# A two-block network on one core: the first block's mixer with float32 projections, modulation vectors as TensorE products, and the whole convolution on VectorE

## The chip, the core and the metric

The kernel runs on one core of a Trainium2 chip: TensorE (PE, with PEld for its weight loads), VectorE (DVE), ScalarE (ACT) and GpSimd (POOL), and one queue of DMA issues on SyncE (SP). The metric is the device time of one execution in microseconds (us); it is given as the median of several runs. A profile is one further execution.

## What is computed

256 tokens of width 1024 go through two blocks. The change touches the first half of the first block, the mixer:

```
mod = silu(c) @ ada_w + ada_b              # 6 vectors of 1024: shift, scale, gate (mixer), shift, scale, gate (ffn)
u   = rmsnorm(x) * (1 + sc_mix) + sh_mix
p   = u @ w_in                             # 8 tiles of 128 columns for the conv, 14 for rwkv
y_conv = silu(layernorm(conv31(a * sigmoid(b)) + b_dw))     # 31 taps, 512 channels, causal
y_rwkv = rwkv7(p_rwkv)                     # decaying 64x64 state per head, group norm, bonus, gate
x   = x + gt_mix * ([y_conv, y_rwkv] @ w_out)
u   = rmsnorm(x) * (1 + sc_ffn) + sh_ffn
x   = x + gt_ffn * peer_ffn(u)             # 8 heads, top 16 of 128 x 128 experts
```

A second block follows (two attention branches, a gated merge and a feed-forward part).

## The kernel before

The tokens are two tiles of 128 (t=0, 1). Each float32 weight tile is loaded by one DMA on SP (512 KB) into a ring (`W_wraw`, three buffers), then split: `wload` casts it to a high part (`W_whi`, on ACT or DVE) and subtracts for a low part (`W_wlo`, on DVE). The activations are split likewise (`Au_uhi`, `Au_ulo`; `Amix_mixhi`, `Amix_mixlo`), and each product is three matmuls in fp32r: high by high, low by high, high by low.

The first block's mixer, called the head here, runs in this order. `norm_T` normalises x and computes `u` for pairs of its eight 128-row blocks. Ahead of each pair, `mods` gets four tiles of the modulation: multiply by silu(c) and sum along the row, three on DVE (`An_mraw`, one instruction with an accumulator) and one on POOL with the sum on ACT. After each pair, `proj_blocks` adds that pair's share of six rwkv tiles ("side", `w_side`). `proj` then does the other eight rwkv tiles (`w_rwkv`) and the eight conv tiles (`w_conv`); each rwkv tile gets its token shift on DVE (`Afeat_xs`). `prep` makes decay, keys and gates. For four chunks of 64 tokens, DVE fills `Ach_W` and `Ach_ZR`, PE multiplies them, and DVE masks the result (`Ach_AB`). The 16x16 blocks on the diagonal go out to DRAM and back (`scrn`, `Ach_nblk`); `base` inverts them on DVE in 15 steps of a multiply (`Ach_ublkp`) and a reduce (`Ach_ublk`); the result goes out (`scrx`) and comes back as `Arw_XT`. `chunk_mats` doubles the inverse in two levels (masked copies COPY_PREDICATED on DVE, `Arw_X`, `Arw_XT`), `chunk_state` carries the state over the chunks (`Arw_VS`, `Arw_S0f`), and `rwkv_out` finishes a token tile: group norm (`Aprep_yr`, `Afeat_gno`), bonus and gate.

`conv` sums 31 taps for four groups of 128 channels into `Afeat_cacc`: group 0 on PE with diagonal matrices (`Arw_cdiag`, 31 float32 matmuls and eight DMAs), groups 1 and 2 on DVE (60 multiply-adds), group 3 as ACT products and POOL sums. The 24 late modulation tiles (vectors 2, 3, 4) are multiplied on DVE or POOL and summed on ACT or DVE. `tok_mm` multiplies by `w_out` (13 tile loads: 8 for t=0, 5 again for t=1), and `E_gtmp` multiplies by the gate. Behind the head come the queries, the top-k and experts of the first block, and the second block.

The order on each engine is fixed ahead of the run by a list scheduler: every operation has a cost, a readiness and a priority (a table of offsets by part, operation and tile), and each engine's queue takes the best ready one. The engines then run their queues strictly in order; so does SP with its DMAs. In the rows of profile and order all operations have one line, that of a helper; names of tiles tell them apart.

## Time and profile before

| | before |
|---|---|
| median of three runs | 1544.62 us (1543.45 to 1553.45) |
| profiled execution | 1536.19 us, span 1534.4 us |
| PE busy | 1413.9 us, 92% |
| DVE busy | 1319.7 us, 86% |
| ACT, POOL busy | 570.0 us, 158.9 us |
| DMA | 305.14 MB, mean 199 GB/s |
| head: last gate multiply of the mixer starts at | 264.18 us |

A busy share says how much of a stretch an engine had work in progress; matmuls are pipelined, so their single durations overlap, and the spacing of their starts is their price.

### The profile page before, as it was taken

Reading aid. Unit: us, or ns where it says so; the run is one execution under the profiler, and the core shown is the slowest. Engines: PE = TensorE matmul, PEld = TensorE weight load, DVE = VectorE, ACT = ScalarE, POOL = GpSimd, SP = SyncE. Lnnn points to the kernel's source line nnn. Section 1 sums busy time; section 2 is a strip of 40 time slices with the busy share of each in tenths; the row PEclk is TensorE's granted clock in tenths of the full one; section 3 lists DMA queues with packets and bytes.
Section 4 is the critical chain, followed back from the end, with each engine's and each line's share of the span. In section 5 each row is a group of like instructions: output and inputs, shape, how many; then the busy total and the mean of one; then the engine's idle time right before and its main releaser. Section 6 shows DMA issues by size and latency. Waiting matters only on the chain.

```text
span 1534.4 us, 24599 instructions
## 1 busy us (share of the span) xinstructions
PE 1413.9 (92%) x9309; PEld 1256.7 (82%) x9309; DVE 1319.7 (86%) x2402; ACT 570.0 (37%) x1019; POOL 158.9 (10%) x127
## 2 busy tenths in 40 slices
...
GB/s 320 252 137 162 165 104 179 230 157 159 114 151 184 134 153 164 174 165 171 208 286 273 303 297 297 293 294 261 197 177 193 157 152 150 221 220 192 193 179 138
DMA packets 99224, 305.14 MB, mean 199 GB/s; under 512 B 17952, under 2 KB 24864, under 8 KB 98976
## 3 DMA queue, kind: packets, MB, share of 16 engines
...
q14 instruction: 47, 0.39, 0.1%
...
## 4 chain that ended last, share of the span: by engine, by line
PE 56%; DVE 24%; DMA 12%; issue 4%; ACT 3%; SPq 0%; POOL 0%; DVEq 0%; ACTq 0%
PE bank L693 56%; DVE W_wlo L693 8%; DVE W_whi L693 2%; DMA W_wraw<-in_peer_v_dram 2%; DVE Afeat_cacc L693 1%; ACT W_whi L693 1%; DMA A_mraw<-in_wmodT_dram 1%; DMA W_wraw<-in_w_out_dram 1%; DMA row<-A_rowcol 1%; DVE Bt_pos L693 1%; DVE Bt_tix L693 1%; DVE Ach_ZR L693 1%; DVE A_mraw L693 1%; DVE Bt_tv L693 1%; DMA row<-C_rowcol 1%
## 5 line engine op out<-in xcount | busy, mean ns | idle before, releaser
L693 DVE TENSOR_TENSOR W_wlo<-W_wraw,W_whi 128x1024 fp32r<-128x1024 f32 (+1 forms) x456 | 560.8, 1236 | 43.4 <-ACT W_whi L693 27.4
L693 ACT CAST W_whi<-W_wraw 128x1024 fp32r<-128x1024 f32 (+1 forms) x238 | 248.8, 1047 | 263.4 <-PE bank L693 162.5
L693 PE MATMUL bank<-X_u2hi,W_wlo 128*128 128x256 f32 x1088 | 302.0, 288 | 12.1 <-DVE W_wlo L693 11.8
L693 PE MATMUL bank<-X_u2hi,W_whi 128*128 128x256 f32 x1088 | 302.6, 287 | 1.7 <-DVE W_whi L693 0.9
L693 PE MATMUL bank<-X_u2lo,W_whi 128*128 128x256 f32 x1088 | 299.7, 285 | 0.0
L693 PEld LDWEIGHTS bank<-X_u2hi,W_wlo 128*128 128x128 f32 x1088 | 205.8, 193 | 15.5 <-DVE W_wlo L693 15.4
L693 DVE CAST W_whi<-W_wraw 128x1024 fp32r<-128x1024 f32 (+1 forms) x218 | 149.4, 686 | 73.1 <-PE bank L693 53.3
L693 PEld LDWEIGHTS bank<-X_u2hi,W_whi 128*128 128x128 f32 x1088 | 206.3, 193 | 2.6 <-DVE W_whi L693 1.5
L693 PEld LDWEIGHTS bank<-X_u2lo,W_whi 128*128 128x128 f32 x1088 | 206.1, 193 | 0.0
L693 PE MATMUL bank<-W_whi,A_ah 128*128 128x512 f32 x512 | 138.7, 390 | 3.9 <-ACT A_ah L693 3.0
L693 PE MATMUL bank<-W_whi,A_al 128*128 128x512 f32 x512 | 139.1, 391 | 1.2 <-DVE A_al L693 1.1
L693 PE MATMUL bank<-W_wlo,A_ah 128*128 128x512 f32 x512 | 138.8, 390 | 1.3 <-DVE W_wlo L693 1.3
L693 PEld LDWEIGHTS bank<-W_whi,A_ah 128*128 128x128 f32 x512 | 95.8, 188 | 25.0 <-ACT A_ah L693 3.6
L693 PEld LDWEIGHTS bank<-W_wlo,A_ah 128*128 128x128 f32 x512 | 95.9, 188 | 22.7 <-DVE W_wlo L693 3.0
L693 PEld LDWEIGHTS bank<-W_whi,A_al 128*128 128x128 f32 x512 | 95.7, 188 | 22.9 <-DVE A_al L693 3.1
L693 ACT CAST A_ah<-gH_gH 128x256 fp32r<-128x256 f32 x128 | 51.2, 406 | 157.7 <-PE bank L693 151.1
L693 PE MATMUL bank<-C_chi,W_wlo 128*128 128x256 f32 (+1 forms) x424 | 106.2, 285 | 0.4 <-DVE W_wlo L693 0.3
L693 PE MATMUL bank<-C_clo,W_whi 128*128 128x256 f32 (+1 forms) x424 | 104.6, 283 | 0.0
L693 PE MATMUL bank<-C_chi,W_whi 128*128 128x256 f32 (+1 forms) x424 | 104.1, 282 | 0.0
L693 DVE SCALAR_TENSOR_TENSOR A_mraw<-A_mraw,A_cvec 128x1024 f32<-128x1024 f32 x56 | 68.3, 1220 | 11.2 <-DMA A_mraw<-in_wmodT_dram 6.0
L693 PEld LDWEIGHTS bank<-C_chi,W_wlo 128*128 128x128 f32 (+1 forms) x424 | 73.8, 187 | 1.8 <-DVE W_wlo L693 1.0
L693 POOL TENSOR_TENSOR C_cosg<-C_rope,C_gains 128x128 f32<-128x128 f32 x8 | 5.6, 730 | 657.9 <-DVE A_mraw L693 652.8
...
## 6 DMA issues: line engine op xcount, KB each, us to landing
W_wraw<-in_peer_u_dram SPq DMA_DIRECT2D x128, 512.0 KB, 3.3
W_wraw<-in_peer_v_dram SPq DMA_DIRECT2D x128, 512.0 KB, 4.5
...
```

The lines of the kernel that those rows point to most:

```text
L693: return getattr(eng, "tensor_copy" if meth == "copy" and e != "ACT" else meth)(*args, **kw)
```

## The change

**Projections.** `u` is kept in float32 (`Au_u`); `u` and the weight tiles of `w_side`, `w_rwkv`, `w_conv` and `w_out` are not split any more. Each product is one float32 matmul from the loaded tile: 176 matmuls with 256 columns in place of 528 in fp32r, and 32 with 512 columns in place of 96. The loads alternate between two rings of three buffers (`Afeat_hraw`, `W_wraw`). `w_out` is loaded once (8 tiles); the conv rows (k 0 to 3) are multiplied first for both token tiles, the rwkv rows (k 4 to 7) for t=0 and then t=1.

**Modulation.** Of the four tiles ahead of a pair, one is now eight float32 products with one column each on PE; three stay on DVE. The late vectors 2, 3 and 4 are eight loads each (`adaR`, 24 in all), each with four matmuls of one output row and 256 columns, which write PSUM partitions 0, 32, 64 and 96; then a copy on ACT, two transposes and one addition on DVE. POOL has no multiplies left in the head.

**Convolution.** All four groups run on DVE: 120 multiply-adds and four first taps. The diagonal matrices and their DMAs are gone.

**Order.** The table of priorities is tuned anew for the whole kernel, and the scheduler's costs of one-row and small matmuls and its rule on POOL and DVE sharing a port are changed. From the queries on, the same instructions remain but for two more table loads on ACT and a few elementwise ones that moved from DVE to POOL; their order differs in places.

The diff, without the table of priorities:

```diff
@@ load and modulation helpers @@
+    def wload32(self, ap, n=1024):
+        self.ring += 1
+        raw = self.T("Afeat", "hraw", [1024], F32, 3) if self.ring % 2 else self.T("W", "wraw", [1024], F32, WRAW)
+        self.nc.sync.dma_start(raw[:, 0:n], ap)
+        return raw[:, 0:n]
+    def mod_products(self, nts, load, tag="m", z=None):
+        nc = self.nc
+        ps = self.psum(tag)
+        for n, nt in enumerate(nts):
+            w = load(self.a["adaN"][nt])
+            for k in range(KT):
+                nc.tensor.matmul(ps[:, n:n + 1], w[:, k * P:(k + 1) * P], self.ccol[:, k:k + 1], start=k == 0, stop=k == KT - 1)
+        return ps
+    def mod_rows(self, i):
+        nc = self.nc
+        ps = self.psum("m")
+        z = self.zero
+        nc.tensor.matmul(ps[:, 0:256], z[:, 0:P], z[:, 0:256], start=True, stop=False)
+        for k in range(KT):
+            w = self.wload32(self.a["adaR"][i, k])
+            for g in range(4):
+                nc.tensor.matmul(ps[32 * g:32 * g + 1, 0:256], self.ccol[:, k:k + 1], w[:, g * 256:(g + 1) * 256], start=False,
+                                 stop=False)
+        nc.tensor.matmul(ps[:, 0:256], z[:, 0:P], z[:, 0:256], start=False, stop=True)
+        rows = self.T("Afeat", "modrows", [256])
+        nc.scalar.copy(rows[:], ps[:, 0:256])
+        pt = self.psum("m")
+        for q in range(2):
+            nc.tensor.transpose(pt[:, q * P:(q + 1) * P], rows[:, q * P:(q + 1) * P], self.ident[:])
+        o = self.mod[:, 0, 8 * i:8 * i + 8].rearrange("p (g q) -> p q g", q=2)
+        b = self.colr("ada_b", 8 * i, 8).rearrange("p (g q) -> p q g", q=2)
+        nc.vector.tensor_add(o, pt[:, 0:256].rearrange("p (q g e) -> p q g e", q=2, e=32)[:, :, :, 0], b)
...
@@ norm_T @@
+        if both:
+            u32 = self.T(oregion, name, [KT, S])
-                nc.any.affine(u[:, q * w:(q + 1) * w], ps[:, q * w:(q + 1) * w], sc[:, k:k + 1], shcol[:, k:k + 1])
+                nc.any.affine(u32[:, k] if both else u[:, q * w:(q + 1) * w], ps[:, q * w:(q + 1) * w], sc[:, k:k + 1], shcol[:, k:k + 1])
+            if both:
+                if split:
+                    nc.scalar.copy(hi[:, sl], u32[:, sl])
+                    nc.vector.tensor_sub(lo[:, sl], u32[:, sl], hi[:, sl].bitcast(F32))
+                after(k0, (u32, hi, lo) if split else (u32,))
+                continue
             uv = u[:].rearrange("p (k t) -> p k t", k=nk)
...
@@ first projections @@
+    def mm_feat(self, ps, ap, u, full, start=True):
+
+        if not full:
+            return self.mm3_feat(ps, self.wload(ap), u[1], u[2])
+        w = self.wload32(ap)
+        for k in range(KT):
+            self.nc.tensor.matmul(ps, w[:, k * P:(k + 1) * P], u[0][:, k], start=k == 0, stop=k == KT - 1)
-            whi, wlo = net.wload(net.a["w_side"][k], SIDE * P)
+            w = net.wload32(net.a["w_side"][k], SIDE * P) if SIDE32 else net.wload(net.a["w_side"][k], SIDE * P)
             for n in range(SIDE):
-                ps = self.pw[n // 2][:, n % 2 * S:(n % 2 + 1) * S]
-                b = slice(n * P, (n + 1) * P)
-                nc.tensor.matmul(ps, whi[:, b], hi[:, k], start=False, stop=False)
-                nc.tensor.matmul(ps, whi[:, b], lo[:, k], start=False, stop=False)
-                nc.tensor.matmul(ps, wlo[:, b], hi[:, k], start=False, stop=k == KT - 1 and n % 2 == 1)
+                ps, b = self.pw[n // 2][:, n % 2 * S:(n % 2 + 1) * S], slice(n * P, (n + 1) * P)
+                sp = k == KT - 1 and n % 2 == 1
+                for x, y in ((w, u[0]),) if SIDE32 else ((w[0], u[1]), (w[0], u[2])):
+                    nc.tensor.matmul(ps, x[:, b], y[:, k], start=False, stop=sp and SIDE32)
+                if not SIDE32:
+                    nc.tensor.matmul(ps, w[1][:, b], u[1][:, k], start=False, stop=sp)
-                net.mm3_feat(half(ps, q), net.wload(w), hi, lo)
+                net.mm_feat(half(ps, q), w, u, RWKV32 if x >= 0 else CONV32)
...
@@ conv @@
-        nc.bias = CONV_BIAS
-        pe = net.psum("x") if CONV_PE else None
-        for k in range(CONV_PE):
-            if k % 4 == 0:
-                dg = net.T("Arw", "cdiag", [4, P], F32, 2)
-                n = min(4, CONV_PE - k)
-                nc.sync.dma_start(dg[:, :n], net.a["conv_diag"][:, k * P:(k + n) * P].rearrange("p (k e) -> p k e", e=P))
-            nc.tensor.matmul(pe[:, :S], dg[:, k % 4], self.convy[:, 0, k:k + S], start=k == 0, stop=k == CONV_PE - 1)
-        nc.bias = 0.0
         nc.bias = TAP_BIAS
         for c in range(4):
-            for k in range(CONV_PE if c == 0 else 0, TAPS):
+            for k in range(TAPS):
                 w = net.col("conv_dw_w", c * TAPS + k)
                 src = self.convy[:, c, k:k + S]
                 if k == 0:
                     nc.vector.tensor_scalar(acc[:, c], src, w, net.col("conv_dw_b", c), op0=OP.mult, op1=OP.add)
-                elif c < CONV_DVE:
-                    nc.vector.scalar_tensor_tensor(acc[:, c], src, w, pe[:, :S] if c == 0 and k == CONV_PE else acc[:, c],
-                                                   op0=OP.mult, op1=OP.add)
                 else:
-                    tp = net.T("Afeat", "tap", [S], F32, 2)
-                    nc.scalar.activation(tp[:], src, AF.Copy, scale=w)
-                    nc.gpsimd.tensor_tensor(acc[:, c], acc[:, c], tp[:], op=OP.add)
-            if c == 0 and CONV_PE:
-                nc.scalar.activation(acc[:, 0], pe[:, :S] if CONV_PE == TAPS else acc[:, 0], AF.Identity, bias=net.col("conv_dw_b", 0))
+                    nc.vector.scalar_tensor_tensor(acc[:, c], src, w, acc[:, c], op0=OP.mult, op1=OP.add)
...
@@ first_mix @@
+    def early(ap):
+        w = net.T("An0", "mraw1", [D], F32, 2)
+        nc.sync.dma_start(w[:], ap)
+        return w
     def mods(k0):
-        net.mod_tiles(0, (k0, k0 + 8, k0 + 1, k0 + 9), FIRST_ENG, "An0", "mraw0", 6)
-        z = lambda ap: ap.rearrange("p (z k) -> p z k", z=2)[:, :, k0:k0 + 2]
-        m = z(net.mod[:, 0, 0:16])
-        net.nc.vector.tensor_add(m, m, z(net.colr("ada_b", 0, 16)))
-    hi, lo = net.norm_T("An0", "Au", net.xs, net.colr("norm_mix_g"), net.mod[:, 0, 0:8], net.mod[:, 0, 8:16], "u", "x",
-                        before=mods, after=mx.proj_blocks)
-    mx.proj(hi, lo)
-    nc = net.nc
-    nc.part = "mods"
-    nc.bias = MOD_BIAS
-    spare = {"c": ("Afeat", "cacc", [4, S]), "y": ("Aprep", "yr", [4, S]), "a": ("Ach", "AB", [4, S], F32, 4)}
-    net.mod_tiles(0, range(16, 16 + MOD_EARLY), MOD_ENG0, spare=[spare[x] for x in MOD_SPARE],
-                  after=net.mod[:, 0, MOD_AFTER:MOD_AFTER + 1])
-    nc.bias = 0.0
+        nts = (k0, k0 + 1, k0 + 8, k0 + 9)
+        if MOD_PE0:
+            ps = net.mod_products(nts[:MOD_PE0], early)
+            for n, nt in enumerate(nts[:MOD_PE0]):
+                nc.vector.tensor_add(net.mod[:, 0, nt:nt + 1], ps[:, n:n + 1], net.colr("ada_b", nt, 1))
+        net.mod_tiles(0, nts[MOD_PE0:], ("vector",), "An0", "mraw0", 5)
+        for nt in nts[MOD_PE0:]:
+            net.mod_bias(0, nt, nt + 1)
+    u = net.norm_T("An0", "Au", net.xs, net.colr("norm_mix_g"), net.mod[:, 0, 0:8], net.mod[:, 0, 8:16], "u", "x",
+                   before=mods, after=mx.proj_blocks, split=not (SIDE32 and RWKV32 and CONV32))
+    mx.proj(u)
     nc.bias = PREP_BIAS
     mx.prep()
     nc.bias = 0.0
@@ -2173,13 +2261,15 @@
     mx.base()
     mx.turn_v()
     M = mx.chunk_mats(0)
+    for i in (2, 3, 4):
+        nc.part = f"mods{i}"
+        nc.bias = MOD_BIAS
+        net.mod_rows(i)
+        nc.bias = 0.0
     mx.bonus()
     mx.conv()
-    nc.part = "mods late"
-    net.mod_tiles(0, range(16 + MOD_EARLY, 40), MOD_ENG)
-    net.mod_bias(0, 16, 40)
-    mx.split_mix(mx.acc, 0, slice(0, S))
     w_out = net.a["w_out"]
+    mix = [mx.acc[:, k] for k in range(4)] + [mx.y[:, k] for k in range(4)]
     for c in range(4):
         M, M1 = mx.chunk_mats(c + 1) if c < 3 else None, M
         nc.bias = STATE_BIAS
@@ -2187,18 +2277,28 @@
         nc.bias = 0.0
         if c == 1:
             mx.rwkv_out(0)
-            mx.split_mix(mx.y, 4, slice(0, P))
         if c == 2:
             mx.ps = [[net.psum(tag) for h in range(2)] for tag in "uv"]
             nc.part = "out0"
-            kept = tok_mm(net, mx.mhi, mx.mlo, w_out, mx.ps, [4, 5, 6, 7, 0, 1, 2, 3], (0,))
+            w = []
+            for k in range(8):
+                w.append(net.wload32(w_out[k]))
+                out_products(net, mix, w, mx.ps, (0, 1) if k < 4 else (0,), (k,))
     nc.bias = OUT_BIAS
     mx.rwkv_out(1)
-    mx.split_mix(mx.y, 4, slice(P, S))
     nc.bias = 0.0
     nc.part = "out1"
-    tok_mm(net, mx.mhi, mx.mlo, w_out, mx.ps, [1, 2, 3, 0, 4, 5, 6, 7], (1,), kept=kept)
+    out_products(net, mix, w, mx.ps, (1,), range(4, 8))
     return mx
+def out_products(net, x, w, ps, tt, ks):
+    for k in ks:
+        for t in tt:
+            for h in range(2):
+                net.nc.tensor.matmul(ps[t][h][:], x[k][:, t * P:(t + 1) * P], w[k][:, h * 512:(h + 1) * 512],
+                                     start=k == 0, stop=k == 7)
```

Where the order moves, on SP first: the end of the base, before. `Ach_ublk` is the base's result, `scrx0` to `scrx3` its four pieces in DRAM, `Arw_XT` the tile it comes back to.

```order
L693 DMA Arw_cdiag_0_1282<-in_conv_diag_dram 128x512
L693 DMA scrx0<-Ach_ublk_0_466 32x16x16
L693 DMA scrx1<-Ach_ublk_0_466 32x16x16
L693 DMA scrx2<-Ach_ublk_0_466 32x16x16
L693 DMA scrx3<-Ach_ublk_0_466 32x16x16
L693 DMA Arw_XT_0_1276<-scrx0 128x4x128
L693 DMA Arw_XT_1_1277<-scrx1 128x4x128
L693 DMA Arw_cdiag_1_1283<-in_conv_diag_dram 128x512
L693 DMA W_wraw_1_82<-in_adaT_dram 128x1024
```

And in the changed kernel; `in_adaR_dram` holds the late modulation weights.

```order
L696 DMA scrx0<-Ach_ublk_0_400 32x16x16
L696 DMA scrx1<-Ach_ublk_0_400 32x16x16
L696 DMA scrx3<-Ach_ublk_0_400 32x16x16
L696 DMA Afeat_hraw_2_109<-in_adaR_dram 128x1024
L696 DMA scrx2<-Ach_ublk_0_400 32x16x16
L696 DMA W_wraw_2_84<-in_adaR_dram 128x1024
...
L696 DMA W_wraw_2_84<-in_adaR_dram 128x1024
L696 DMA Afeat_hraw_2_109<-in_adaR_dram 128x1024
L696 DMA W_wraw_1_83<-in_adaR_dram 128x1024
L696 DMA Arw_XT_0_923<-scrx0 128x4x128
L696 DMA Arw_XT_1_924<-scrx1 128x4x128
L696 DMA W_wraw_0_82<-in_adaR_dram 128x1024
```

Before, the two reads of `scrx` follow the four writes directly; now twelve loads of `adaR` stand between the write of `scrx0` and its read.

On DVE, from the last base steps to the first masked copies, before (`Afeat_cacc` is the convolution's sum):

```order
L693 TENSOR_TENSOR Ach_ublkp_0_467<-Ach_ublk_0_466,Ach_nblk_0_465 128x225
L693 TENSOR_REDUCE Ach_ublk_0_466<-Ach_ublkp_0_467 128x15
L693 SCALAR_TENSOR_TENSOR Afeat_cacc_0_105<-Afeat_convy_0_104,G_cols_0_72,Afeat_cacc_0_105 128x256
...
L693 COPY Arw_VS_0_1270<-bank3_63 64x4x64
L693 TENSOR_TENSOR Aprep_av_0_120<-bank0_60,Afeat_xs_0_103 128x512
...
L693 TENSOR_SCALAR Afeat_cacc_0_105<-Afeat_convy_0_104,G_cols_0_72 128x256
L693 TENSOR_SCALAR Aprep_av_0_120<-Aprep_av_0_120,G_cols_0_72 128x256 x4
L693 SCALAR_TENSOR_TENSOR Aprep_yr_0_119,G_mod_0_77<-Aprep_yr_0_119,Afeat_cvec_0_93 128x1024
...
L693 COPY_PREDICATED Arw_X_0_1274<-Afeat_clev_0_95,bank4_64 128x16x16
L693 COPY_PREDICATED Arw_XT_0_1276<-Afeat_clev_0_95,bank3_63 128x16x16
L693 SCALAR_TENSOR_TENSOR Afeat_cacc_0_105<-Afeat_convy_0_104,G_cols_0_72,Afeat_cacc_0_105 128x256
L693 COPY_PREDICATED Arw_XT_0_1276<-Afeat_clev_0_95,bank3_63 128x8x32
```

And in the changed kernel:

```order
L696 TENSOR_TENSOR Ach_ublkp_0_401<-Ach_ublk_0_400,Ach_nblk_0_399 128x225
L696 TENSOR_REDUCE Ach_ublk_0_400<-Ach_ublkp_0_401 128x15
L696 TENSOR_SCALAR Afeat_cacc_0_111<-Afeat_convy_0_106,G_cols_0_72 128x256 x2
L696 SCALAR_TENSOR_TENSOR Afeat_cacc_0_111<-Afeat_convy_0_106,G_cols_0_72,Afeat_cacc_0_111 128x256 x11
...
L696 SCALAR_TENSOR_TENSOR Afeat_cacc_0_111<-Afeat_convy_0_106,G_cols_0_72,Afeat_cacc_0_111 128x256 x36
L696 TENSOR_TENSOR Afeat_convy_0_106<-bank0_60,Au_convsg_1_139 128x256
L696 TENSOR_SCALAR Afeat_cacc_0_111<-Afeat_convy_0_106,G_cols_0_72 128x256
...
L696 COPY Arw_VS_1_918<-bank4_64 64x4x64
...
L696 SCALAR_TENSOR_TENSOR Afeat_cacc_0_111<-Afeat_convy_0_106,G_cols_0_72,Afeat_cacc_0_111 128x256 x17
L696 COPY_PREDICATED Arw_X_0_921<-Afeat_clev_0_97,bank4_64 128x16x16
L696 SCALAR_TENSOR_TENSOR Afeat_cacc_0_111<-Afeat_convy_0_106,G_cols_0_72,Afeat_cacc_0_111 128x256 x4
L696 COPY_PREDICATED Arw_XT_0_923<-Afeat_clev_0_97,bank3_63 128x16x16
```

Two of the convolution's multiply-adds stood ahead of the third masked copy; now 66 stand ahead of the first one, and the others lie between the masked copies, state copies and sums that follow.

On PE, around the transposes of the second token tile's group norm (`Afeat_gno`), before:

```order
L693 MATMUL bank4_64<-W_whi_1_85,Amix_mixhi_0_1265 128x512
L693 MATMUL bank3_63<-W_whi_1_85,Amix_mixhi_0_1265 128x512
L693 MATMUL bank0_60<-G_ident_0_74,Afeat_gno_0_115 128x128 x4
L693 MATMUL bank4_64<-W_wlo_0_87,Amix_mixhi_0_1265 128x512
L693 MATMUL bank3_63<-W_wlo_0_87,Amix_mixhi_0_1265 128x512
L693 MATMUL bank4_64<-W_whi_1_85,Amix_mixlo_0_1266 128x512
L693 MATMUL bank3_63<-W_whi_1_85,Amix_mixlo_0_1266 128x512
L693 MATMUL bank4_64<-W_whi_0_84,Amix_mixhi_0_1265 128x512
```

And in the changed kernel:

```order
L696 MATMUL bank0_60<-Afeat_cmask_0_96,Afeat_gsq_0_115 128x8 x4
L696 MATMUL bank3_63<-W_wraw_0_82,Aprep_yr_0_130 128x512
...
L696 MATMUL bank4_64<-W_wraw_2_84,Aprep_yr_0_130 128x512
L696 MATMUL bank3_63<-W_wraw_2_84,Aprep_yr_0_130 128x512
L696 MATMUL bank2_62<-G_ident_0_74,Afeat_gno_0_119 128x128 x4
L696 MATMUL bank6_66<-Afeat_hraw_1_108,Afeat_cacc_0_111 128x512
...
L696 MATMUL bank5_65<-W_wraw_1_83,Afeat_cacc_0_111 128x512
L696 MATMUL bank6_66<-Afeat_hraw_0_107,Aprep_yr_0_130 128x512
L696 MATMUL bank5_65<-Afeat_hraw_0_107,Aprep_yr_0_130 128x512
...
L696 MATMUL bank5_65<-W_wraw_2_84,Aprep_yr_0_130 128x512
```

Before, split products of t=0 (banks 3 and 4) lie on both sides of the transposes; now all of t=0 stands in front of them, and 12 float32 products of t=1 (banks 5 and 6) behind, the last eight with `Aprep_yr`.

## Rows read from the trace of the kernel before

**Rows 1.** Page, part 1: busy us (share of the span) and instructions.

```profile
PE 1413.9 (92%) x9309; PEld 1256.7 (82%) x9309; DVE 1319.7 (86%) x2402; ACT 570.0 (37%) x1019; POOL 158.9 (10%) x127
```

**Rows 2.** Stretches: length; busy us of PE, PEld, DVE, ACT, POOL; clock.

```profile
0.00:57.20 57.20, 24.43 (x150) 21.63 (x151) 44.27 (x87) 20.20 (x36) 12.22 (x14) 1.00 0.81 295
57.20:123.00 65.80, 56.53 (x390) 53.00 (x389) 63.99 (x108) 36.00 (x60) 12.44 (x15) 0.95 0.54 181
...
152.00:200.00 48.00, 46.00 (x471) 41.07 (x472) 30.97 (x54) 33.10 (x68) 38.30 (x25) 1.00 0.56 177
200.00:228.00 28.00, 18.54 (x96) 14.42 (x96) 26.33 (x67) 5.04 (x10) 0.00 (x0) 0.63 0.18 53
228.00:265.00 37.00, 31.39 (x132) 23.68 (x131) 33.36 (x56) 18.14 (x29) 1.05 (x1) 0.91 0.54 180
265.00:1534.00 1269.00, 1219.92 (x7962) 1087.76 (x7962) 1096.62 (x1982) 444.49 (x794) 75.69 (x53) 0.99 0.60 201
```

**Rows 3.** Group on DVE, 0 to 265 us: count | busy, mean ns.

```profile
L693 DVE MEMSET Ach_ZR<- 128x1024 f32 x4 | 3.6, 912 | 0.6 <-issue 0.5
```

**Rows 4.** Stretch, DVE on tiles W_wlo and W_whi alone (casts, splits).

```profile
57.20:123.00 65.80, 16.62 (x15) 0.95 0.54 181
```

**Rows 5.** DVE in order of time (start, length), 44 to 58 us.

```profile
44.73 1.22 DVE L693 SCALAR_TENSOR_TENSOR An_mraw<-An_mraw,Afeat_cvec 128x1024 f32<-128x1024 f32 x1
...
57.27 0.88 DVE L693 SCALAR_TENSOR_TENSOR Afeat_xs<-bank,Afeat_omu,Au_shift 128x256 f32<-128x256 f32 x2
```

**Rows 6.** PE in order of time, 42 to 44 us.

```profile
42.04 0.84 PE L693 MATMUL bank<-Au_uhi,W_whi 128*128 128x256 f32 x3
...
43.56 0.28 PE L693 MATMUL bank<-Au_ulo,W_whi 128*128 128x256 f32 x1
43.68 0.29 PE L693 MATMUL bank<-Au_uhi,W_wlo 128*128 128x256 f32 x1
```

**Rows 7.** DVE in order of time, 122 to 184 us.

```profile
122.26 0.68 DVE L693 TENSOR_TENSOR Ach_AB<-bank,Afeat_cmask 128x512 f32<-128x512 f32 x1
...
133.34 0.80 DVE L693 TENSOR_TENSOR Ach_ublkp<-Ach_ublk,Ach_nblk 128x1 f32<-128x1 f32 x1 [2.21 <-DMA Ach_nblk<-scrn]
...
137.84 0.17 DVE L693 TENSOR_TENSOR Ach_ublkp<-Ach_ublk,Ach_nblk 128x16 f32<-128x16 f32 x1
...
138.93 0.57 DVE L693 TENSOR_TENSOR Ach_ublkp<-Ach_ublk,Ach_nblk 128x36 f32<-128x36 f32 x1
...
150.84 0.39 DVE L693 TENSOR_REDUCE Ach_ublk<-Ach_ublkp 128x15 f32<-128x225 f32 x1
...
162.33 0.44 DVE L693 COPY_PREDICATED Arw_X<-Afeat_clev,bank 128x256 f32<-128x256 uint8 x1 [0.70 <-PE bank L693]
...
183.49 0.69 DVE L693 TENSOR_TENSOR Aprep_yr<-Aprep_yr,bank 128x512 f32<-128x512 f32 x1
```

**Rows 8.** POOL in order of time, 136 to 153 us.

```profile
136.24 16.84 POOL L693 TENSOR_TENSOR Afeat_cacc<-Afeat_cacc,Afeat_tap 128x256 f32<-128x256 f32 x19 [2.12 <-DVE Ach_ublkp L693]
```

**Rows 9.** SP's queue in order of time, 122 to 131 us.

```profile
122.97 0.38 SPq L693 DMA_DIRECT2D scrn<-Ach_AB  x1
...
130.06 0.33 SPq L693 DMA_DIRECT2D Ach_nblk<-scrn  x1
```

**Rows 10.** DVE in order of time, 200 to 266 us.

```profile
201.20 13.54 DVE L693 SCALAR_TENSOR_TENSOR Afeat_cacc<-Afeat_convy,G_cols,Afeat_cacc 128x256 f32<-128x256 f32 x34
...
225.23 0.68 DVE L693 TENSOR_TENSOR Aprep_yr<-Aprep_yr,bank 128x512 f32<-128x512 f32 x1
...
264.18 1.28 DVE L693 TENSOR_TENSOR E_gtmp<-bank,E_row 128x512 f32<-128x512 f32 x2
```

**Rows 11.** PE in order of time: float32 products, 256 columns and 1 column.

```profile
193.42 1.03 PE L693 MATMUL bank<-Afeat_convy,Arw_cdiag 128*128 128x256 f32 x4
194.28 0.27 PE L693 MATMUL bank<-G_ident,Afeat_gno 128*128 128x128 f32 x1
...
230.29 2.91 PE L693 MATMUL bank<-Afeat_o,Afeat_convy 128*128 128x1 f32 x16 [1.67 <-ACT Afeat_convy L693]
```

893 lines of the change are left out of this document (469 added, 424 removed).

## The prediction

> **What bounds the kernel now.** I read the busy shares first. PE is busy 92% of the span and DVE 86% [rows 1], which looks like a PE-bound kernel; by stretch it is not so. From 265 us to 1534 us PE works 1219.9 of 1269 us [rows 2], and the change leaves those instructions as they are. In the head PE works 24.4 of the first 57.2 us, while DVE works 44.3; from 57.2 to 123 us DVE works 64.0 of 65.8 us; from 200 to 228 us DVE works 26.3 of 28 while PE works 18.5 at a granted clock of 0.63 [rows 2]. So the head is led by DVE and by chains that pass through it, and only its last 37 us, where PE works 31.4, are led by PE.
>
> Then I took DVE in order of time and noted when each stage ends: the first token shift at 57.27, the last masked AB at 122.26, the base from 133.34 to 151.23, the first masked copy at 162.33, the mean subtraction of the first group norm at 183.49 [rows 5, 7]; the same of the second group norm at 225.23 and the last gate multiply at 264.18 [rows 10]. The sum below moves these marks one by one.
>
> **The first shift.** What goes: the fp32r casts and splits of `u` and `w_side`, which ended between the last modulation multiply at 44.73 and the shift at 57.27 [rows 5]. What stays: sixteen modulation tiles of 0.52 MB, eight side tiles of 0.39 MB and about 1.5 MB of inputs, 13 MB. The stretch moved 295 GB/s [rows 2], at which 13 MB take 44 us. DVE has 12 of the 1.2 us multiplies left and almost nothing between them, so the data sets the pace. PE adds 32 one-column products: eight of them took 2.91 us [rows 11], 11.6 us in all, in a stretch in which it idles 33. The 48 side products in float32 cost 0.43 us each (two of them, four records, from 193.42 to 194.28 [rows 11]), and only the last pair's twelve, 5 us, lie behind the last modulation tile. I take 45 us: 12 saved, or 6 if the side products run at the half speed that split ones showed up to 43 us (three in 0.84 us, against starts 0.12 us apart just behind [rows 6]).
>
> **From the shift to the base.** DVE's 64.0 us held 16.6 of weight casts and splits [rows 4] and, as the program has it, five late modulation multiplies of 1.2 us. Without both it has 41. Three of the four ZR clears of 0.9 us [rows 3] go to POOL: 38 to 39. PE must put through 47 float32 projections (20 us), eight lora and sixteen ZR by W products of the same form (10 us) and small ones before the last AB: about 36 us, nearly as much. Table loads on ACT and two engines so close in length will not fit without a gap; I take 43 us for the stage and keep the 11.1 us from the last AB to the first base step, of which the write to `scrn` took 7.1 until its read was issued [rows 7, 9]. Base start: 45 + 43 + 10 = 98, against 133.34. Saved in this stage 23, with ends of 27 (39 us) and 15.
>
> **The base.** It took 17.9 us for 15 steps. While POOL summed the convolution from 136.24 to 153.08 [rows 8], a multiply of 36 elements took 0.57 us and one of 16 just before took 0.17 [rows 7]; the casts and other work in between took some 4 us. POOL has nothing left to do then. At 0.17 us and a little for the longer steps, 15 pairs take 7 to 9 us; I take 9, which saves 9. The other end is 14 us, if the two multiplies of `Afeat_convy` that stand ahead of step 15 wait: their 32 float32 products, 14 us, start behind the last AB product at about 88 and end near 103, when step 15 is due. Base end: 107 against 151.23.
>
> **Base to first group norm.** Here the change gives time back. All of the convolution now stands on DVE between the base and that subtraction: 120 multiply-adds, 0.396 us apart (34 of them from 201.20 to 214.66 [rows 10]), and four first taps of about 0.5: 49.5 us. That is the price of taps back to back while POOL rests, as it does in the changed kernel. Twenty-odd other instructions there (six masked copies of 0.44 [rows 7], state copies, sums, bonus) make 13 us. DVE has 63 us in a row and comes to the subtraction at 170; before it took 32.3. Lost: 31, or 36 with waits at the small ones. The late modulation hides under this: 24 loads of 0.52 MB take 43 us at 295 GB/s, from about 107 to 150, and `Arw_XT`, behind twelve of them on SP, lands at about 128. DVE does not reach the first masked copy before 66 taps and four first taps are done, 107 + 28 + 3 = 138, so ten microseconds cover it. If that cover were gone, every further microsecond would move the chunk chain.
>
> How long the one-row products take no row shows. Serially, 96 of 0.43 us are 41 us on PE; if the four that go to different partitions run side by side, 10 us. PE has some 60 us here and little else, so I charge nothing, but at the upper end each load's four take 1.7 us and the loads go no slower than the 1.8 us that their DMA takes. The Trainium skill, TensorEngine Tiling (Array Packing), section Key Properties, says that tiles operate independently and can multiply in parallel, and also that changing the tiling mode drains TensorE; by the first the 96 cost 10 us, by the second each return to full-width products adds a drain that no row of this trace prices. The sum is the same by either.
>
> **First to second group norm.** Before: 41.7 us, of which 53 taps took 21 on DVE, in front of state copies. None are left, so 21 remain for the two last chunks. PE has 24 float32 w_out products of 512 columns in there or just behind, 0.85 us each by twice the 256 column price: 20 us, of which I let 6 fall on the chain. 27 us: 15 saved, between 8 and 20.
>
> **Second group norm to the last gate multiply.** Before: 39.0 us, during which split w_out products kept PE full and five weight tiles were split. Now: about 6 us until the normalised tile is ready (an estimate: a dozen small steps on DVE, ACT and PE, 0.2 to 0.7 us each), five products ahead of its transposes (4 us, partly under it), twelve behind them at 0.85, 10 us; the first four, with convolution rows, cover the 3 us of bonus and gate. 19 us at full clock, 33 at half; PE falls to 0.63 in a like stretch, 200 to 228 us [rows 2]. I take 22: 17 saved, between 6 and 20. The Trainium skill, TensorE: Matmul & The Clock Gate, section What's actually happening, has it that the throttled state is the default and that activity releases it; by that alone the products would start at half speed wherever PE waits for the state chain, and the end would lie near 33 us, not 22. Rows of this case show both: 0.63 where DVE held the chain, 0.91 from 228 on.
>
> **The sum.** 12 + 23 + 9 - 31 + 15 + 17 = 45. I have costed each stage as if its longest engine ran without gaps; before, even the stretch full of taps idled 6% and the chunk stretch, 152 to 200, idled 17 of 48 us on DVE [rows 2]. Six per cent of the 125 us from the first shift to the first group norm are 8 us, so the head ends 37 us sooner. Against the profiled execution's 1536.2 us that is 1499; the median of the runs was 1544.6, and on that scale it is 1508.
>
> **Rivals.** *The convolution on DVE takes back most of the gain* (small gain). For: 49.5 us of taps in an in-order queue ahead of masked copies, with `Arw_XT` behind twelve loads on SP. If one-row products run serially at half clock, 3.4 us a load, twelve loads end at 148, not 128, and the first masked copy at 150, not 138; with state copies waiting behind taps for 8 us more, the gain is 37 - 20 = 17: 1528. Against: the taps themselves fill the wait.
>
> *The tail pays.* Its order is retuned; PE idles 49 of 1269 us there [rows 2], so at most 49 can be won, and an order that adds a third to this idle time loses 16: 1524. Against: instruction counts and the load order there hardly differ.
>
> *Slower: float32 products on a half-speed PE.* From the shift to the last AB, PE needs 36 us at full clock and DVE 39; at half clock PE needs 72 and leads. Then the base starts at 127 in place of 98, `convy` comes 14 us later still, the last stage takes 33 us in place of 22: 29 + 14 + 11 = 54, and the result is 1508 + 54 = 1562. It decides from about 50 us of float32 work at half clock, since 37 are then used up. For: the half speed up to 43 us [rows 6]. Against: the clock is 0.95 in this stage [rows 2], and PE will be busier in it than before.
>
> *No effect.* The marks move, but the clock or waits take about 35 us at the head's end: 1543.
>
> **Chances.** My forecast, gain of 22 to 55 us: 0.60. More than that: 0.05. Small gain or a paying tail: 0.19, about half of it over 1%. No effect: 0.08. Slower: 0.08. One per cent, about what a measurement here can tell from no change, is 15 us; faster by more: 0.75, within: 0.17, slower by more: 0.08. The best ends of all terms (12, 27, 10, -28, 20, 20) sum to 61; the worst (6, 15, 4, -36, 8, 6) to 3: 1484 to 1541 holds a little over eight tenths.
>
> **What would show it.** In the new profile: first shift at 45, last AB at 88, base from 98 to 107, the masked copy near 138 behind taps, the two subtractions at 170 and 197, the last gate multiply near 225; group of taps 0.40 us each; no POOL multiply in the head; and the stretch behind the head as long as before, 1269 us. The forecast is wrong if PE's clock lies near 0.5 before 100 us, if a masked copy waits for `Arw_XT`, or if that last stretch changes by over 10 us.

## The result and the profile after

The changed kernel takes 1504.51 us (median of four, 1502.66 to 1507.02) against 1545.6 beside it: a ratio of 0.973, interval 0.970 to 0.976, 41 us faster. The prediction said 1508, between 1484 and 1541, and faster by over 1% with a chance of 0.75. The profiled execution took 1507.02 us, span 1505.2. Its page, part 1, and the first line of its chain of waits:

```profile
PE 1432.8 (95%) x9307; PEld 1252.0 (83%) x9307; DVE 1258.5 (84%) x2395; ACT 511.3 (34%) x917; POOL 97.8 (6%) x91
...
PE 72%; DVE 14%; DMA 9%; ACT 3%; issue 2%; SPq 0%; POOL 0%; DVEq 0%; ACTq 0%; POOLq 0%
```

By stretches (length; busy us of PE, PEld, DVE, ACT, POOL; granted clock, DMA share, GB/s), cut where the stages end now:

```profile
0.00:43.50 43.50, 33.33 (x163) 28.88 (x164) 25.45 (x78) 10.10 (x21) 9.25 (x16) 1.00 0.94 367
43.50:96.00 52.50, 50.81 (x242) 43.19 (x241) 43.88 (x92) 21.77 (x39) 2.61 (x14) 1.00 0.52 153
96.00:106.00 10.00, 10.00 (x48) 8.81 (x47) 9.00 (x33) 0.38 (x1) 0.00 (x0) 1.00 0.35 118
106.00:181.00 75.00, 63.52 (x577) 44.80 (x576) 60.09 (x153) 14.03 (x32) 0.00 (x0) 0.95 0.68 227
181.00:213.00 32.00, 32.00 (x264) 23.91 (x263) 14.03 (x38) 12.47 (x22) 0.00 (x0) 0.95 0.15 50
213.00:232.00 19.00, 19.00 (x60) 9.44 (x58) 12.20 (x29) 3.02 (x8) 0.00 (x0) 1.00 0.22 63
232.00:1505.00 1273.00, 1224.13 (x7964) 1092.98 (x7962) 1093.87 (x1978) 449.58 (x796) 85.91 (x61) 0.99 0.62 201
```

Before, DVE led most of the head [rows 2]; now each stretch has its own leader: DMA up to 43.5 us (0.94 busy), PE from there to the base, and PE again from 181 us on (51 of 51 us). Only from 106 to 181 us is no engine full: PE 63.5 of 75, DVE 60.1, DMA 0.68. The question behind the result lies there. DVE in order of time shows the marks that the prediction named:

```profile
43.48 0.88 DVE L696 SCALAR_TENSOR_TENSOR Afeat_xs<-bank,Afeat_omu,Au_shift 128x256 f32<-128x256 f32 x2 [1.11 <-ACT Au_shift L696]
...
85.12 2.48 DVE L696 TENSOR_TENSOR Ach_AB<-bank,Afeat_cmask 128x512 f32<-128x512 f32 x4
...
96.00 0.16 DVE L696 TENSOR_TENSOR Ach_ublkp<-Ach_ublk,Ach_nblk 128x1 f32<-128x1 f32 x1 [2.32 <-DMA Ach_nblk<-scrn]
...
98.06 0.22 DVE L696 TENSOR_TENSOR Ach_ublkp<-Ach_ublk,Ach_nblk 128x36 f32<-128x36 f32 x1
...
105.39 0.39 DVE L696 TENSOR_REDUCE Ach_ublk<-Ach_ublkp 128x15 f32<-128x225 f32 x1
...
132.46 6.92 DVE L696 SCALAR_TENSOR_TENSOR Afeat_cacc<-Afeat_convy,G_cols,Afeat_cacc 128x256 f32<-128x256 f32 x17
141.26 0.45 DVE L696 COPY_PREDICATED Arw_X<-Afeat_clev,bank 128x256 f32<-128x256 uint8 x1 [1.88 <-PE bank L696]
...
180.28 0.69 DVE L696 TENSOR_TENSOR Aprep_yr<-Aprep_yr,bank 128x512 f32<-128x512 f32 x1 [4.27 <-PE bank L696]
...
212.81 0.69 DVE L696 TENSOR_TENSOR Aprep_yr<-Aprep_yr,bank 128x512 f32<-128x512 f32 x1 [1.98 <-PE bank L696]
...
230.45 0.69 DVE L696 TENSOR_TENSOR E_gtmp<-bank,E_row 128x512 f32<-128x512 f32 x1 [0.60 <-PE bank L696]
```

They answer to [rows 5, 7, 10]. At the masked copy and at both group norms DVE now waits for PE, where the prediction had PE wait for DVE's taps.

What PE and SP did around `Arw_XT` (the base's result, read back), in order of time:

```profile
126.98 3.19 PE L696 MATMUL bank<-Au_u,W_wraw 128*128 128x256 f32 x14
130.11 0.61 PE L696 MATMUL bank<-W_wraw,G_ccol 128*1 128x256 f32 x8
...
134.91 0.63 PE L696 MATMUL bank<-G_ident,Arw_XT 128*128 128x128 f32 x4 [0.68 <-DMA Arw_XT<-scrx]
...
150.71 0.61 PE L696 MATMUL bank<-Afeat_hraw,G_ccol 128*1 128x256 f32 x8 [1.90 <-DMA Afeat_hraw<-in_adaR_dram]
151.14 0.61 PE L696 MATMUL bank<-W_wraw,G_ccol 128*1 128x256 f32 x8
151.68 0.94 PE L696 MATMUL bank<-Arw_X,Ach_AB 128*128 128x128 f32 x6
...
162.17 1.10 PE L696 MATMUL bank<-Arw_R,Arw_XT 128*128 128x64 f32 x8
...
168.11 1.00 PE L696 MATMUL bank<-Arw_R,Arw_XT 128*128 128x64 f32 x8
...
176.39 1.06 PE L696 MATMUL bank<-G_ident,Arw_XT 128*128 128x128 f32 x4 [3.40 <-DMA Arw_XT<-scrx]
...
178.95 1.29 PE L696 MATMUL bank<-Aprep_yr,Afeat_bd 128*128 128x128 f32 x6
```

```profile
130.25 0.93 SPq L696 DMA_DIRECT2D Arw_XT<-scrx  x2
...
163.31 0.38 SPq L696 DMA_DIRECT2D Arw_XT<-scrx  x1
...
169.14 0.36 SPq L696 DMA_DIRECT2D Arw_XT<-scrx  x1
```

The base ends at 105.8, but `Arw_XT` is read only at 130.25: its memory opens when the last product that reads `Au_u` has ended (126.98 + 3.19 = 130.17). In e5, e6, e7, e9 and e10 below, where that product ends at other times, the read follows it by the same 0.08 us. That wait is not in the prediction. The products, in turn, stand in PE's queue among the one-row products of the late modulation (`G_ccol` rows): seven groups of four stand ahead of the last one.

The two later reads wait in the same way, for the tiles of the first two chunks. They go out at 163.31 and 169.14, as the chunk products that read those tiles (`Arw_R<-Arw_XT`) end: 162.17 + 1.10 and 168.11 + 1.00. PE then waits 3.40 us for the last of them at 176.39, and the sums of the first group norm (178.95) stand behind it in PE's queue: that is the norm's wait of 4.27 us.

### The profile page after: what moved, and what is told of

It reads as the page before. It is cut to its first block, busy times and chain, and to the rows that moved or that the text cites. A ratio compares the mean times of both kernels' runs of the same rounds, so it can differ in the third digit from the quotient of the medians.

```text
span 1505.2 us, 24345 instructions
## 1 busy us (share of the span) xinstructions
PE 1432.8 (95%) x9307; PEld 1252.0 (83%) x9307; DVE 1258.5 (84%) x2395; ACT 511.3 (34%) x917; POOL 97.8 (6%) x91
## 4 chain that ended last, share of the span: by engine, by line
PE 72%; DVE 14%; DMA 9%; ACT 3%; issue 2%; SPq 0%; POOL 0%; DVEq 0%; ACTq 0%; POOLq 0%
PE bank L696 72%; DVE W_wlo L696 4%; DMA W_wraw<-in_peer_v_dram 2%; ACT W_whi L696 1%; DMA W_wraw<-in_w_gua_dram 1%; DVE W_whi L696 1%; DMA row<-A_rowcol 1%; DMA Arw_XT<-scrx 1%; DMA row<-C_rowcol 1%; DVE Ach_ZR L696 1%; DMA W_wraw<-in_w_out_dram 1%; DVE Bt_tv L696 1%; DMA W_wraw<-in_peer_u_dram 1%; DVE Bt_tix L696 1%; DVE Bt_pos L696 1%
## 5 line engine op out<-in xcount | busy, mean ns | idle before, releaser
L696 DVE TENSOR_TENSOR W_wlo<-W_wraw,W_whi 128x1024 fp32r<-128x1024 f32 x417 | 515.8, 1241 | 40.4 <-ACT W_whi L696 21.8
L696 PE MATMUL bank<-X_u2hi,W_wlo 128*128 128x256 f32 x1088 | 295.4, 287 | 8.5 <-DVE W_wlo L696 8.3
L696 ACT CAST W_whi<-W_wraw 128x1024 fp32r<-128x1024 f32 x217 | 227.6, 1050 | 222.7 <-PE bank L696 128.1
L696 PE MATMUL bank<-X_u2hi,W_whi 128*128 128x256 f32 x1088 | 296.7, 287 | 3.6 <-ACT W_whi L696 2.9
L696 PE MATMUL bank<-X_u2lo,W_whi 128*128 128x256 f32 x1088 | 293.7, 285 | 0.0
L696 DVE CAST W_whi<-W_wraw 128x1024 fp32r<-128x1024 f32 x202 | 139.5, 691 | 88.2 <-PE bank L696 60.5
L696 PEld LDWEIGHTS bank<-X_u2hi,W_wlo 128*128 128x128 f32 x1088 | 202.7, 193 | 11.2 <-DVE W_wlo L696 11.1
L696 PEld LDWEIGHTS bank<-X_u2hi,W_whi 128*128 128x128 f32 x1088 | 203.1, 193 | 5.3 <-ACT W_whi L696 4.1
L696 PEld LDWEIGHTS bank<-X_u2lo,W_whi 128*128 128x128 f32 x1088 | 202.9, 193 | 0.0
L696 PE MATMUL bank<-W_wlo,A_ah 128*128 128x512 f32 x512 | 139.9, 392 | 0.0
L696 PEld LDWEIGHTS bank<-C_chi,W_whi 128*128 128x128 f32 (+1 forms) x424 | 73.6, 187 | 0.8 <-ACT Ca_sg L696 0.2
```

The source lines that it names most:

```text
L696: return getattr(eng, "tensor_copy" if meth == "copy" and e != "ACT" else meth)(*args, **kw)
```

## The experiments

Each was timed beside the kernel before; medians and ranges in us, ratio to before with its 95% interval, and from the profile the starts of the first masked copy, of the first group norm's subtraction and of the last gate multiply.

```
                       median (range)             ratio [interval]        masked  norm   gate
after                  1504.51 (1502.66-1507.02)  0.973 [0.970, 0.976]    141.3  180.3  230.5
e1_taps16              1496.18 (1494.47-1498.93)  0.967 [0.965, 0.970]    143.0  185.2  228.8
e2_conv0_pe            1512.01 (1510.33-1517.24)  0.977 [0.975, 0.980]    138.6  198.8  246.2
e3_xt_first            1510.35 (1508.12-1513.68)  0.977 [0.974, 0.979]    136.4  195.4  241.2
e4_mods_tiles          1526.96 (1523.13-1529.52)  0.987 [0.984, 0.990]    138.5  158.7  253.3
e5_taps16_same         1501.42 (1499.39-1502.47)  0.971 [0.968, 0.975]    141.7  179.8  229.3
e6_conv4_same          1494.73 (1490.85-1497.67)  0.967 [0.963, 0.971]    142.5  178.9  227.7
e7_both_same           1496.55 (1490.76-1501.15)  0.970 [0.966, 0.973]    139.9  175.4  224.8
e8_wout4_same          1494.69 (1490.90-1499.21)  0.968 [0.964, 0.972]    141.6  178.6  225.4
e9_mods_off_same       1487.17 (1486.22-1490.74)  0.963 [0.960, 0.965]    135.9  168.8  216.8
e10_mods_conv_off      1487.54 (1484.94-1491.69)  0.963 [0.960, 0.965]    137.3  170.4  219.4
e11_sub16              1513.27 (1508.45-1515.08)  0.978 [0.975, 0.980]    143.8  192.6  240.9
e12_before_conv_dve    1568.15 (1566.38-1572.93)  1.014 [1.012, 1.016]    192.4  214.2  292.9
```

e1 to e4, e11 and e12 were planned anew, so their orders move in places. e5 to e10 keep the changed kernel's order: an instruction is planned and given its place, but not issued. The marks are from one profile each and scatter: e8 changes nothing ahead of the first group norm, and that comes 1.7 us sooner there. Behind the last gate multiply e5 to e10 take 3 to 11 us less than the changed kernel, with the same instructions in the same order, so medians and marks are told apart below.

### Do the taps hold the head? e1, e5

The theory of the prediction (A): 49.5 us of taps set the way from the base to the first group norm.

```diff
-            for k in range(TAPS):
+            for k in range(16):
```

> The changed kernel, but with the first 16 of the 31 taps of each channel group left out of nothing else: the other 15 are not computed, so 60 of the 120 multiply-adds on DVE are gone (60 x 0.396 = 24 us). Theory A (the convolution on DVE sets the pace between the base and the first group norm): that subtraction, 180.3 us in the changed kernel, comes 12 to 20 us sooner, and the time falls from 1504.5 to about 1487 (1483 to 1494). Rival B (PE, the 24 loads of late modulation weights and the reads of XT behind them set it, and the taps only fill the waits): XT still lands at about 135 us, and the time falls by less than 5 us.

The taps ended at 147 instead of 176 us, and the last gate multiply came 1.6 us sooner; the masked copy and the norm came later. The median fell by 8, in neither range, and nearly all of it behind the head. The new plan, which sends the later reads of `Arw_XT` only from 172.49 us on, blurs this, so the same taps were left out in the old order:

```diff
                 else:
+                    if k >= 16:
+                        SKIP.add(len(nc.ops))
                     nc.vector.scalar_tensor_tensor(acc[:, c], src, w, acc[:, c], op0=OP.mult, op1=OP.add)
```

> The changed kernel with its order on every engine kept, and taps 16 to 30 of each channel group not issued: 60 multiply-adds, 24 us, fewer on DVE. (The first experiment left out the same taps but let the scheduler plan anew.) Theory C: the first XT read can't be issued before the last projection, since its tile lies in memory that the projections' u occupies; the read went out at 130.25 us, just behind the last projection on PE (126.98 + 3.19). Then the first masked copy stays at 139 to 141 us, and the head ends 3 to 9 us sooner, by taps between the later masked copies only: 1496 to 1502. Theory A (DVE's taps ahead of the masked copy are the bound): masked copy near 128, head 15 to 20 us sooner, 1485 to 1490.

DVE of that run in order of time:

```profile
128.83 0.42 DVE L699 TENSOR_TENSOR Afeat_convy<-bank,Au_convsg 128x256 f32<-128x256 f32 x1 [9.05 <-ACT Au_convsg L699]
...
141.69 0.45 DVE L699 COPY_PREDICATED Arw_X<-Afeat_clev,bank 128x256 f32<-128x256 uint8 x1 [1.79 <-PE bank L699]
...
155.92 0.45 DVE L699 COPY_PREDICATED Arw_XT<-Afeat_clev,bank 128x256 f32<-128x256 uint8 x1 [6.76 <-PE bank L699]
```

Where the taps were, DVE idles (9.05 and 6.76 us), and nothing behind moves beyond the scatter: the norm at 179.8 against 180.3, the last gate multiply 1.2 us sooner. The median, 3 us lower, is at the edge of C's range. A falls; something that ends on PE holds the stage.

### Trading DVE work against PE work: e2, e3

```diff
+        if CONV_PE:
+            pe = net.psum("x")
...
+                nc.tensor.matmul(pe[:, :S], dg[:, k % 4], self.convy[:, 0, k:k + S], start=k == 0, stop=k == TAPS - 1)
```

> The changed kernel with the first channel group of the convolution back on PE (31 float32 products with diagonal matrices, 8 loads), the other three groups on DVE: 30 multiply-adds and a first tap less on DVE (12 us), 13 us more on PE, 2 MB more to load. Theory A: 4 to 9 us faster than the changed kernel, 1496 to 1500. Rival B: no faster, since the second pair of reads of XT now stands behind loads of diagonal matrices that wait for PE; 1503 to 1512.

It is 7.5 us slower than the changed kernel: the taps end at 169 instead of 176, but the norm comes at 198.8. It went as B had it: loads of the diagonal matrices stand ahead of the last read of `Arw_XT`, which goes out at 186.34 instead of 169.14. So the run does not tell what relief for DVE alone is worth. Next, `Arw_XT` ahead of late modulation loads on SP, by priority:

```diff
-    "mats0 dma_start XT": 5000.0,
+    "mats0 dma_start XT": 400000.0,
...
-    "mats1 dma_start XT": 6000.0,
+    "mats1 dma_start XT": 400000.0,
```

> The changed kernel with the four reads of XT given the highest priority in the scheduler, so that four loads of late modulation weights and not twelve stand ahead of the first pair. Theory A: the PE waits for XT in the changed kernel (0.68 us at 134.9 and 3.40 us at 176.4) go, with up to 5 us: 1500 to 1503. Rival B: the first pair comes sooner but DVE reaches the masked copies no sooner, behind 66 taps; the time stays within 2 us, 1503 to 1506, and the second pair's wait goes on, since it waits for the tile and not for the queue.

The masked copy came 5 us sooner, the norm 15 us later, the median 6 higher, outside both ranges. The loads that were passed over (19 instead of 12 of the 24 now stand behind the read) met the later chunks: PE waits 4.92 us for one at 164.91, and the later reads of `Arw_XT` go out from 175.83 on.

### Products or loads? e6, e7, e8

```diff
         for k in range(KT):
+            if skip and 2 <= k < 6:
+                SKIP.add(len(self.nc.ops))
             self.nc.tensor.matmul(ps, w[:, k * P:(k + 1) * P], u[0][:, k], start=k == 0, stop=k == KT - 1)
```

> The changed kernel with its order kept and half of the convolution's input projections (row blocks 2 to 5 of 8, 32 float32 products, 13.7 us of PE) not issued; their loads stay. Theory C: the last projection ends and the XT read goes out 8 to 13 us sooner (117 to 122 in place of 130), but 66 taps still stand ahead of the first masked copy on DVE, which comes at 135 to 139; the head ends 2 to 6 us sooner, 1498 to 1503. Theory A: XT sooner, the time unchanged within 2 us.

PE of that run:

```profile
110.89 0.37 PE L699 MATMUL bank<-Afeat_zero 128*128 128x256 bf16 x1 [4.29 <-DVE Afeat_xs L699]
...
118.84 0.61 PE L699 MATMUL bank<-W_wraw,G_ccol 128*1 128x256 f32 x8 [1.79 <-DMA W_wraw<-in_adaR_dram]
...
123.96 0.61 PE L699 MATMUL bank<-W_wraw,G_ccol 128*1 128x256 f32 x8 [1.65 <-DMA W_wraw<-in_adaR_dram]
...
125.75 1.46 PE L699 MATMUL bank<-Au_u,W_wraw 128*128 128x256 f32 x6
130.51 0.61 PE L699 MATMUL bank<-W_wraw,G_ccol 128*1 128x256 f32 x8 [3.29 <-DMA W_wraw<-in_adaR_dram]
```

32 products of 0.43 us (13.7 us) are gone, yet the last one ends at 127.2, 3 us sooner. The rest went into waits of PE: 4.77 us at 103.90 for DVE's `Afeat_convy`, 4.29 at 110.89 for DVE's token shift, which stands behind 11 taps, and 3.4 for tiles of the late modulation (`adaR`), whose one-row products stand ahead of the projections. With so much idle time the granted clock is 0.51, near the lower of its two levels (1.2 of 2.4 GHz), from 104 to 112 us, against 0.98 in the changed kernel. The masked copy comes no sooner (142.5), the last gate multiply 2.8 us sooner; the median fell by 10, most of it behind the head. The expectation missed, and a new theory (D) came from it: the 24 loads and 96 one-row products, not the taps, hold this stage. e7 leaves out both the products of e6 and the taps of e5:

> Both of the two before: 60 taps and 32 convolution projections not issued, same order. If two nearly equal chains (DVE's taps; PE's projections, then the XT read) run side by side up to the first masked copy, leaving out both gains more than the sum of each alone: masked copy at 122 to 130, head 14 to 22 us sooner, 1483 to 1491. If there were one chain, both together give what the better one gives alone, within 3 us.

The first expectation missed: the masked copy stays at 139.9. The second was met: with both left out the median is within 2 us of e6 alone, the last gate multiply within 3 us. Neither the taps nor the projections' products hold the masked copy, as D would have it. e8 leaves out half of the w_out products (k = 2, 3, 5, 6), for the last stage:

> The changed kernel with its order kept and w_out's products for row blocks 2, 3, 5 and 6 not issued: 16 of 32 float32 products with 512 columns, 13.7 us at 0.857 us each; loads stay. Theory P (from the end of the convolution at 195 us to the last gate multiply at 231 us PE is the bound: it was busy 28.0 of 28.0 us from 200 to 228): the head ends 9 to 13 us sooner, 1492 to 1496. Rival S (the state chain of the last two chunks and the second group norm set it): less than 5 us.

The median lies in P's range, but the last gate multiply came 5 us sooner, not 9 to 13, and only 3.3 of them behind the first group norm; the rest came behind the head. By the marks S holds. With the products gone, PE waits for DVE's bonus and gate steps, 3.03 us at 219.47, and its granted clock is 0.83 from 208 to 228 us: the two products that follow at 219.47 take 1.68 us each instead of 0.86. So the run does not separate what PE's work costs there from what its clock does.

### The late modulation taken away: e9, e10

```diff
         for k in range(KT):
+            if k:
+                SKIP.add(len(nc.ops))
             w = self.wload32(self.a["adaR"][i, k])
             for g in range(4):
+                if k:
+                    SKIP.add(len(nc.ops))
```

> The changed kernel in its own order, but 21 of the 24 late modulation tiles are neither loaded nor multiplied (84 of the 96 one-row products): those vectors are wrong, and the time is that of a kernel without their loads. Theory D (behind the base the queues of SP and TensorE are paced by these loads: XT can't be read before the last float32 projection, and one-row products that wait for their tile stand ahead of that projection): the last projection ends at 119 to 123 us instead of 130.2, XT is read there, the first masked copy starts at 130 to 135 instead of 141.3, and the head ends 5 to 11 us sooner: 1493 to 1500 us. Rival (the chain through the convolution's gate and its taps on VectorE holds the masked copy whatever the loads do): the projections end sooner but the first masked copy stays at 138 to 142 and the time within 3 us of 1504.5.

By far the largest step: 17 us in the median, 11.5 at the norm, 13.6 at the last gate. The same 63 us on both, first the changed kernel, then e9, and DVE of e9 in order of time:

```profile
106.00:169.00 63.00, 55.02 (x510) 37.09 (x508) 52.46 (x135) 12.12 (x28) 0.00 (x0) 0.97 0.78 265
```

```profile
106.00:169.00 63.00, 53.23 (x412) 44.63 (x411) 58.66 (x153) 13.84 (x32) 0.00 (x0) 0.92 0.32 95
...
129.03 6.92 DVE L699 SCALAR_TENSOR_TENSOR Afeat_cacc<-Afeat_convy,G_cols,Afeat_cacc 128x256 f32<-128x256 f32 x17
135.87 0.42 DVE L699 COPY_PREDICATED Arw_X<-Afeat_clev,bank 128x256 f32<-128x256 uint8 x1
...
168.85 0.68 DVE L699 TENSOR_TENSOR Aprep_yr<-Aprep_yr,bank 128x512 f32<-128x512 f32 x1
```

Now DVE works 58.7 of 63 us, the masked copy follows the taps without a gap, and the norm comes at 168.85 with no wait in front. Here, by DVE's rows, the taps do lead; no run leaves out taps and late modulation together. D named the cause, but its numbers missed: the last projection ends at 126.3, not 119 to 123, and only 5.4 us are won up to the masked copy. Six more come between it and the norm, where the later `Arw_XT` reads are issued at 152.75 and 161.06 instead of 163.31 and 169.14, and two behind the norm. e10 takes the products of e6 out as well:

> As the run before it, and 32 of the 64 products of the convolution's projections are not issued as well (their sums are wrong). Theory D: with the loads out of the way the products count, which without that gave only 3 us: the last projection ends at 112 to 117, the first masked copy starts at 122 to 129, and the head ends 9 to 18 us sooner than in the changed kernel: 1486 to 1495 us. Rival (VectorE's own queue, base and taps, is next right behind): the masked copy starts no sooner than in the run before it, and the time is the same as there within 3 us.

No further gain: the rival holds. The last projection ends at 120.9, still not at 112 to 117, and then PE waits 4.38 us for DVE's `Afeat_convy`, which stands behind the first taps: DVE is next. So two ways, 11 us apart, meet at the first group norm, one through the late modulation (180), one through the taps (169 to 170), and shortening either alone shows only what the other leaves. Whether loads or one-row products weigh more in the first way was not separated: e6 shows PE waiting 6.7 us for the loads, while in the changed kernel PE waits for them 2.1 us in this stage.

### What the other parts are worth: e4, e11, e12

The late vectors as tiles on DVE and POOL, as before:

```diff
-    for i in (2, 3, 4):
...
-        net.mod_rows(i)
...
+    net.mod_tiles(0, range(16, 40), ("vector", "gpsimd"))
+    net.mod_bias(0, 16, 40)
```

> The changed kernel with the 24 late modulation tiles computed the old way, by turns as one multiply-and-sum on DVE (12 x 1.22 us = 15 us) and as a multiply on POOL (12 x 2.4 us) with the sum on ACT. Theory A (DVE is the bound in this stretch): 15 to 28 us slower than the changed kernel, since the DVE work adds to the taps and POOL's multiplies slow them: 1520 to 1532. Rival B (it would have hidden here as well, and the gain came from elsewhere): less than 6 us slower.

22 us slower, as A said: the first group norm comes 22 us sooner, but the second 22 us later (234.8), since most taps and tiles now stand between them. Its stretch 160 to 200 us, and twelve tiles on DVE:

```profile
160.00:200.00 40.00, 12.83 (x68) 10.17 (x68) 39.92 (x93) 7.05 (x13) 13.00 (x4) 0.63 0.22 79
...
L696 DVE SCALAR_TENSOR_TENSOR W_wraw<-W_wraw,Afeat_cvec 128x1024 f32<-128x1024 f32 x12 | 17.1, 1429 | 6.4 <-DMA W_wraw<-in_adaT_dram 6.4
```

DVE is full, PE works 12.8 of 40 us, and its granted clock is 0.63. The one-row products, though they hold the stage now, are the cheaper form. Then DVE's half of the weight splits put back (the products stay float32):

```diff
         w = self.wload32(ap)
+        lo = self.T("W", "wlo", [1024], F32R, 3)
+        self.nc.vector.tensor_tensor(lo[:], w, w, op=OP.subtract)
```

> The changed kernel with the VectorE half of the weight splits put back: for each of the sixteen projection tiles one 128x1024 subtraction into a spare tile that nothing reads; the products stay float32. Theory A (the splits on VectorE paced the head up to the base, as the prediction has it): sixteen of 1.2 us are 19 us, of which the roughly 9 us that VectorE idles between 45 and 100 us hide half: the last masked AB moves from 87.6 to 95 to 105 and the time to 1513 to 1523 us. Rival (TensorE's float32 products pace this stretch by now, 53 of 55 us): the subtractions hide, the last AB moves by less than 4 us and the time is 1504 to 1508 us.

9 us slower, at A's lower edge, but not as A had it: the last AB stays at 88.2. Only four of the sixteen subtractions stand ahead of it; three follow up to 93 us, and nine come at 102.6 or later, as DVE shows:

```profile
102.61 1.22 DVE L696 TENSOR_TENSOR W_wlo<-W_wraw 128x1024 fp32r<-128x1024 f32 x1
...
114.97 1.22 DVE L696 TENSOR_TENSOR W_wlo<-W_wraw 128x1024 fp32r<-128x1024 f32 x1 [0.75 <-DMA W_wraw<-in_w_conv_dram]
...
119.74 2.46 DVE L696 SCALAR_TENSOR_TENSOR Afeat_cacc<-Afeat_convy,G_cols,Afeat_cacc 128x256 f32<-128x256 f32 x6
```

The taps in a row start at 119.7 instead of 106.3, 13 us later and 2 more than the other way leaves room for. The norm comes 12 us later, with 40 taps right ahead of it (176.79 to 192.7); how much of that is the new order is open.

Last, the convolution alone, in the kernel before:

```diff
-CONV_DVE = 3
-CONV_PE = 31
+CONV_DVE = 4
+CONV_PE = 0
```

> The kernel before with only its convolution changed: all four groups of taps on VectorE, none on TensorE or GpSimd, everything else as before. Theory A (the move costs VectorE time where it leads and gives back only the base, where GpSimd's sums slowed VectorE): 62 more taps of 0.40 us are 25 us, less about 9 us in the base: 1555 to 1566 us; a 36-element multiply of the base then takes about 0.22 us instead of 0.57. Rival (taps fill waits in the head, and the base gains as much as they cost): within 5 us of 1545.

21.5 us slower, 2 us beyond A's range. The base did not gain; it took 40 us in place of 17.9. DVE there, and POOL:

```profile
144.26 0.20 DVE L693 TENSOR_TENSOR Ach_ublkp<-Ach_ublk,Ach_nblk 128x25 f32<-128x25 f32 x1
...
144.72 2.19 DVE L693 TENSOR_TENSOR Ach_ublkp<-Ach_ublk,Ach_nblk 128x36 f32<-128x36 f32 x1
...
161.97 2.12 DVE L693 TENSOR_TENSOR Ach_ublkp<-Ach_ublk,Ach_nblk 128x144 f32<-128x144 f32 x1
164.12 0.30 DVE L693 TENSOR_REDUCE Ach_ublk<-Ach_ublkp 128x12 f32<-128x144 f32 x1
164.46 2.15 DVE L693 TENSOR_TENSOR Ach_ublkp<-Ach_ublk,Ach_nblk 128x169 f32<-128x169 f32 x1
```

```profile
141.63 2.35 POOL L693 TENSOR_TENSOR W_wraw<-W_wraw,Afeat_cvec 128x1024 f32<-128x1024 f32 x1 [1.83 <-DMA W_wraw<-in_adaT_dram]
144.49 2.34 POOL L693 TENSOR_TENSOR W_wraw<-W_wraw,Afeat_cvec 128x1024 f32<-128x1024 f32 x1 [0.51 <-DMA W_wraw<-in_adaT_dram]
...
158.89 15.00 POOL L693 TENSOR_TENSOR W_wraw<-W_wraw,Afeat_cvec 128x1024 f32<-128x1024 f32 x6 [1.84 <-DMA W_wraw<-in_adaT_dram]
```

The sums were POOL's work no longer, but late modulation tiles of 2.3 to 2.5 us (15.00 for six) took their place. Seven of the 15 multiplies of the base begin while POOL multiplies, and six of them take 2.1 to 2.3 us: 2.19 us for the 36 elements that take 0.22 in the changed kernel. One that falls between two of POOL's keeps its 0.20 (25 elements at 144.26), and the reduces are untouched. All 15 together take 16.1 us against 8.2 before. That is 8 of the 22 us by which the base grew. The larger part is other work and waits that the new plan put between its steps: 9.3 us lie between the ninth reduce (149.58) and the tenth multiply (158.87), 4.53 of them a wait for the convolution's gate. PE's granted clock is 0.58 from 135 to 175.5 us, against 0.87 from 125 to 152 in the kernel before. Moved alone, in this plan, the convolution costs; another place for the late modulation on POOL was not tried.

## Why the prediction was right, and where its steps were off

**First shift, 45: 43.5.** Data sets the pace as it said (DMA 0.94 busy). That the time fits is in part luck: the stretch moved 16 MB, not 13, at 367 GB/s rather than 295.

**To the base, 88 and 98: 87.6 and 96.0.** Right in size. The reason was half right: up to the last AB DVE works 37.9 us, as the 38 to 39 had it, but PE works 42.4 of 44.1, not 36, and leads. e11 doesn't settle it, since only four of its subtractions came ahead of the last AB; they did not move it.

**Base, 9 us: 9.8.** Right: with POOL at rest the 36-element multiply takes 0.22 us. The multiplies take 4.5 us together instead of 8.2; the other 4 are the work in between that is gone, as forecast. e12 shows from the other side what POOL does to the multiplies.

**Base to first group norm, 63 us: 74.5.** The step that failed is "The late modulation hides under this", with "`Arw_XT`, behind twelve of them on SP, lands at about 128". The read did not wait for the twelve loads but for the last float32 projection, which stands behind one-row products in PE's queue; it was issued at 130.25 and first used at 134.91. The two later reads, which the prediction does not cost at all, waited for tiles too and went out at 163.31 and 169.14. Without the late modulation the stage takes 168.85 - 105.8 = 63 us (e9), the price given for the taps. So the term was right for one of two ways, and the other was 11 us longer. The one-row products themselves cost near the lower of the two prices: 10 to 13 us for the 96 by the starts of their groups (see the last section). By its own sign of being wrong, "if a masked copy waits for `Arw_XT`", the forecast failed here: the first masked copy waits 1.88 us for PE, which had waited 0.68 us for that tile.

**First to second group norm, 27 us: 32.5; 9 us won, not 15.** PE is full there (32.0 of 32): twelve of the sixteen products with convolution rows of w_out, 10.3 us, run ahead of the second norm, where 6 were allowed. From 181 to 190 us, behind the wait of 3.40 us, the granted clock is 0.82, which the term left out. What set the stage stays open: e8 leaves out four of the twelve, 3.4 us, and the stage is 1.1 us shorter.

**Last stage, 22 us: 17.6; 21 us won, not 17.** PE ran at full clock, 1.00, so the allowance for a slower one was not needed. The prediction had set a rule of the Trainium skill (TensorE: Matmul & The Clock Gate, What's actually happening), that the throttled state is the default and activity releases it, against this step. PE was busy without a gap for 32 us ahead of it, and the slow start of 33 us did not come; where PE had waited, in e8, the clock was 0.83 and the products slow. The slower rival falls with it: up to 104 us, where most of the float32 work is, the granted clock is 1.00, the upper of the two levels. Only the first four float32 products, from 20.36 to 23.35 us, start 0.64 to 0.86 us apart instead of 0.43, though the granted clock reads 1.00 there too.

**The sum.** By the profiles the head ends 33.7 us sooner (264.18 to 230.45) where 37 were forecast; the terms added to 45. Missing are 11 at the norm and 6 between the norms, won are 4 at the end and 2 at the first shift. The allowance of 8 us, made for gaps in busy engines, covered most of this; that it did is luck, since the loss came from a wait and not from gaps. By the medians the gain is 41. The profiled execution of before lay 8 to 9 us below its median and that of after 2.5 above, so the other 7 us are either the stretch behind the head or scatter. That stretch took 1270.2 us before and 1274.7 after in the profiles, and, from the same last multiply, 1264 to 1271 in e5 to e10, where its instructions stand in the same order. It stays open; the rival *the tail pays*, which needed 16 us there, has no support. That the 37 us won up to the base come from the float32 projections is read from the profiles; no run puts the split products back.

No version here beats the changed kernel with the whole work done. e9 bounds what hiding the late modulation better could bring: about 14 us in the head, 17 in the median. Recording two of its vectors later was not tried.
